# A decoder layer with 32 experts: the first 15 expert chunks are issued from GpSimd's queue, and the other chunk buffers are taken in another order

## The chip, the core and the metric

The kernel runs on one core of a Trainium2 chip. The metric is the time of one execution on the device, in microseconds (us). The median of three runs of the kernel before is 767.46 us (767.24 to 767.67). Engines are named as in the profile: PE is TensorE, PEld its weight loads, DVE is VectorE, ACT is ScalarE, POOL is GpSimd, SP is SyncE. A "q" behind a name (SPq) is the engine's instruction queue, from which DMAs are issued among other things.

## The reference, cut to what matters

One decoder layer on 512 tokens of width 1024. Three token mixers (attention over the 128 best keys that an indexer picks, a causal convolution, attention over 256 memory tokens) are projected, gated, added and multiplied by `w_o`. Behind them stands a mixture of 32 experts, of which each token takes two:

```
g_sel = argmax(h @ w_rg + b_rg)                    # one of 4 groups
top_v, top_i = top_k(e_in, 2)                      # 2 of its 8 experts
for n in range(N_EXPERTS):
    a, b = split(h @ w_up[n], 2)                   # w_up[n]: 1024 x 512
    out = out + combine[:, n] * ((silu(a) * b) @ w_down[n])   # w_down[n]: 256 x 1024
```

The weights of the experts are 32 x 6 chunks of 128 x 1024 numbers in float32, 512 KB each, some 100 MB in all. Every one of them is read once.

## The kernel before

**Stages.** `build` writes the program for all engines in source order; a scheduler then sets the order in each engine's queue by its own estimate of when an instruction can go, and puts in the waits. Each queue is worked off strictly in its order. The stages that matter here, with the time at which they run: attention A (`a_s1`, `a_s2`, lines 670 to 726) up to 414; its projection (`proj_units`, L441 to L449) up to 437; the output projection `w_o` (lines 841 to 857) up to 493; the router and the lists of tokens (lines 885 to 983) up to 512; and the experts (lines 1229 to 1252) to the end.

**Weights of the mixers** are loaded by `raw_w` (L132) on SP's queue into 3 buffers `w`; `split_w` cuts each into a high part `wh` (ACT, L127) and a low part `wl` (DVE, L128), with 3 buffers each. A load has to wait until the split of the chunk three before it has read its buffer.

**Expert chunks.** `seq` (L759) lists all 192 chunks in the order in which PE uses them: for each of 16 pairs of experts, three times two up chunks, the four down chunks of the pair before, and the last two up chunks. `slots` is a ring of 42 buffers of 512 KB, made from `RINGS` (L84): 6 of `w3`, 9 of `w1`, 4 of `ot`, 4 of `mg`, 3 of `w`, 3 of `wh`, 3 of `wl`, 2 of `xc`, 3 of `hw`, 2 of `hx`, 1 of `wg`, 2 of `s5`. Chunk n goes to slot n mod 42. These are no extra memory: each lies where earlier stages kept something, and its DMA waits until the last reader of that is done. `w3` (pool `rp`) lies over the queries, keys and values of attention A; `w1` (pool `ea`) over that stage's gates, scores and scratch; `ot` over the inputs of the projections; `mg` over the merged branches; `w`, `wh` and `wl` are the buffers of the mixers' weights; `xc` holds x for the residual; `hw` and `hx` the inputs of `w_o`; `wg` the router's scratch; `s5` what is written out per column of `w_o`.

**Who issues what.** `fetch` (L772) issues chunks, all from SP (L779): 23 at L805, ahead of the loop over `w_o`; 11 at L866, behind it; the rest of the first 42 at L1225, with `behind=first`, which makes the two `s5` chunks wait for the list of tokens (L777, a copy on POOL). From chunk 42 on, a chunk is issued when `expert_raw` asks for it, and waits until PE has used up the chunk 42 before it.

**POOL** does little: it raises to the power -0.5 (L146, L887), clears `zz` (L808; the matmul of L809 reads it) and two tiles for gathered tokens (L995), gathers each pair's tokens from `h2d` (L999), adds the results into the output (L1156) and loads one pair of chunks anew (L1197).

**Between `w_o` and the experts** PE runs `busy_pe(24)` (L983, matmuls of L863) ahead of the transposes of the first gathered tokens (L1137) and of the first up matmul (L1165).

Of the kernel before, what the change touches and what calls it, by code (L numbers as in the profile page):

```python
# [67 lines left out]
for _name, _w in (("g_mix", KD), ("g_mem", KD), ("b_gate", 24), ("conv_b", 4), ("ln_g", 4), ("ln_b", 4),  # L68
# [11 lines left out]
RING = 3  # L80
RING_A = 9
RING_B = 6
SPLIT = 3
RINGS = (("w3", RING_B), ("w1", RING_A), ("ot", 4), ("mg", 4), ("w", RING), ("wh", SPLIT), ("wl", SPLIT), ("xc", 2),  # L84
         ("hw", 3), ("hx", 2), ("wg", 1), ("s5", 2))
CONV_LOW = 1500
TOPK_LOW = 900

# [1 line left out]
def build(nc, tc, I, O, dbg=None):  # L90
    V, A, G, T, SY = nc.vector, nc.scalar, nc.gpsimd, nc.tensor, nc.sync
    es = ExitStack()
    with es:
# [36 lines left out]
        def raw_w(*key):  # L130
            w = wpool.tile([P, 1024], F32, name="w", tag="w")
            SY.dma_start(w, I["wp"][W_KEYS.index(key)])  # L132
            return w

        def split_w(w, n=1024):
            wh = spool.tile([P, 1024], F32R, name="wh", tag="wh")
            wl = spool.tile([P, 1024], F32R, name="wl", tag="wl")
            split_into(wh[:, :n], wl[:, :n], w[:, :n])
            return wh, wl
# [113 lines left out]
        for k in range(KD):  # L253
# [14 lines left out]
            wh, wl = split_w(kv_raw[k] if k < RING else raw_w("kv", k))  # L268
# [477 lines left out]
        def expert_at(e):  # L746
            return nc.values_load(ordi[0:1, e:e + 1], engines=(mybir.EngineType.SP,), min_val=0, max_val=NE - 1,
                                  skip_runtime_bounds_check_because="an index of 32 values")

        def chunk(e, c):  # L750

            if e in EARLY:
                return I["we"][e, c]
            if e not in at_pos:
                at_pos[e] = expert_at(e)
            return I["we"][bass.ds(at_pos[e], 1), c].rearrange("o p n -> (o p) n")
# [8 lines left out]
            if j is not None and j != NW:  # L765
                seq += [(e, 3) for e in pair(j)]
        pools = dict(ot=hp, hw=hp, hx=hp, w3=rp, xc=rp, w1=ea, w=wpool, wh=spool, wl=spool, s5=ea, wg=ea, mg=mpool)
        slots = [tag for tag, n in RINGS for _ in range(n)]
        bufs = {tag: slots.count(tag) for tag in slots}
        fetched, used = [], [0]  # L770

        def fetch(count, behind=None):  # L772
            for n in range(len(fetched), min(len(fetched) + count, len(seq))):
                tag = slots[n % len(slots)]
                w = pools[tag].tile([P, 1024], F32, name="we", tag=tag, bufs=bufs[tag])
                if behind is not None and tag == "s5":
                    G.tensor_copy(w[:, 0:1], behind[:, 0:1])  # L777
                e, c = seq[n]
                SY.dma_start(w, chunk(e, c))  # L779
                fetched.append(w)  # L780

        def expert_raw(e, c):
            n = used[0]
            assert seq[n] == (e, c)
            used[0] += 1
            if len(fetched) <= n:
                fetch(n + 1 - len(fetched))
            w, fetched[n] = fetched[n], None
            return w

        def eat(tag, name, bufs=1, dt=F32):
            return ea.tile([P, 1024], dt, name=name, tag=tag, bufs=bufs)
# [10 lines left out]
        out_v = O["out"][0:S, :].rearrange("(t p) d -> p t d", p=P)  # L803
        h2d_v = h2d.rearrange("(t p) d -> p t d", p=P)
        fetch(RING_B + RING_A + 4 + 4)  # L805
        lg = sct("lg")
        zz = eat("s4a", "zz")
        G.memset(zz[:, 0:148], 0.0)  # L808
        T.matmul(lg[:, 0:148], zz[:, 0:P], zz[:, 0:148], start=True, stop=False)  # L809
        lists = pvt("lists")  # L810

# [29 lines left out]
        for c in range(KD):  # L841
            ps = mmt("wo")
            wh, wl = split_w(wo_raw[c])
# [20 lines left out]

        busy_pe(5, xs[:, 512:1024])
        fetch(RING + 2 * SPLIT + 2)  # L866


# [4 lines left out]
        def r3(name, *dims, at=None, dt=F32):  # L873
            n = int(np.prod(dims))
            if at is None:
                at = taken[0]
                taken[0] += n
            assert at + n <= 1024
            t_ = scr[:, at:at + n]
            if dt is not F32:  # L880
                t_ = t_.bitcast(dt)
            ax = " ".join(f"a{i}" for i in range(len(dims)))
            return t_, t_.rearrange(f"p ({ax}) -> p {ax}", **{f"a{i}": d_ for i, d_ in enumerate(dims)})
# [4 lines left out]
        _, L = r3("lgs", NT, 36)  # L888
# [6 lines left out]
        _, pr = r3("pr", NT, NG)  # L895
# [13 lines left out]
        _, oh = r3("oh", NT, 2, NE)  # L909
# [15 lines left out]
        _, rk = r3("rk", NT, 2, NE)  # L925
# [476 lines left out]
```

## Time and profile before

| | us |
|---|---|
| median of 3 runs | 767.46 |
| the profiled execution | 766.1 |
| its span, from the first to the last instruction | 764.2 |
| PE busy | 717.2 (94%) |
| DVE busy | 477.5 (62%) |
| ACT busy | 266.3 (35%) |
| POOL busy | 90.8 (12%) |
| bytes by SP's DMA queue (q1) | 147.74 MB |
| bytes by POOL's DMA queue (q0) | 8.46 MB |

Busy time of PE is an upper bound of its work, since the ends of matmuls are modelled and a matmul that overlaps the next counts in full. The DMA share is the mean busy share of 16 DMA engines; it can come out a little above 1. All times within the span count from its start.

### The profile page before, as it was taken

How to read it: one execution, taken by the hardware profiler on the slowest of the kernel's cores; microseconds unless marked ns; L12 is line 12 of the kernel's file. 1: busy time of each engine (PE TensorE's matmuls, PEld its weight loads, DVE VectorE, ACT ScalarE, POOL GpSimd, SP SyncE). 2: the span in 40 equal slices, each digit the busy share in tenths (PEclk: the TensorE clock that was granted, in tenths of full speed). 3: DMA queues.
4: the chain of work that ended last, by engine and by line, in shares of the span. 5: the costliest groups of instructions: out<-in, count | busy, mean ns of one | idle time of the engine just before them, and what ended most of it. 6: DMA issues, size and time to landing. Idle time of an engine off the chain costs nothing. (4 is left out here: it accounts for less than half of the span.)

```text
span 764.2 us, 10080 instructions
## 1 busy us (share of the span) xinstructions
PE 717.2 (94%) x3468; PEld 477.9 (63%) x3468; DVE 477.5 (62%) x1085; ACT 266.3 (35%) x503; POOL 90.8 (12%) x82
## 2 busy tenths in 40 slices
PE   6999999999999999999998999989999998889882
PEld 5778888887878778888776888834333333233220
DVE  5879989999999999999986844272112112111100
ACT  6722254455633376237775422101111111000100
POOL 1110010011000050000000000021226322100010
PEclk9999999999999999999999999999999999999997
DMA  9632221213222222321214799999999999999982
GB/s 357 232 121 82 88 79 55 82 58 111 83 83 83 83 84 72 98 80 55 84 55 150 273 378 340 329 315 377 400 378 359 354 370 387 361 381 395 391 324 49
DMA packets 56684, 161.13 MB, mean 211 GB/s; under 512 B 9508, under 2 KB 17956, under 8 KB 56624
## 3 DMA queue, kind: packets, MB, share of 16 engines
q1 hardware_dynamic: 42320, 147.74, 52.2%
q0 software_dynamic: 6624, 8.46, 4.8%
q10 hardware_dynamic: 7680, 4.20, 1.9%
q8 instruction: 29, 0.48, 0.2%
q14 instruction: 31, 0.25, 0.1%
HBM read 162.93 MB, written 13.11 MB: 230 GB/s over the span
## 5 line engine op out<-in xcount | busy, mean ns | idle before, releaser
L1165 PE MATMUL up<-we,xt 128*64 128x512 f32 x544 | 140.8, 599 | 5.4 <-DMA we<-in_we 5.4
L127 ACT CAST wh<-w 128x1024 fp32r<-128x1024 f32 (+2 forms) x75 | 78.3, 1046 | 80.4 <-PE proj L314 22.2
L128 DVE TENSOR_TENSOR wl<-w,wh 128x1024 fp32r<-128x1024 f32 (+2 forms) x75 | 90.9, 1213 | 13.0 <-ACT wh L127 11.2
L1165 PEld LDWEIGHTS up<-we,xt 128*64 128x64 f32 x544 | 39.1, 136 | 77.5 <-issue 59.1
L328 DVE SCALAR_TENSOR_TENSOR y<-u,conv_wh,y 128x512 f32<-128x512 f32 x120 | 84.2, 745 | 0.3
L1155 DVE COPY y<-dn 128x512 f32<-128x512 f32 x17 | 11.8, 692 | 108.9 <-PE dn L1179 108.9
L1179 PE MATMUL dn<-we,acth 128*64 128x512 f32 x272 | 73.5, 596 | 0.6 <-issue 0.6
L314 PE MATMUL gate<-h,wh 128*128 128x512 f32 x240 | 67.9, 397 | 0.0
L1154 ACT COPY y<-dn 128x512 f32<-128x512 f32 x17 | 10.0, 586 | 123.7 <-PE dn L1179 72.7
L1179 PEld LDWEIGHTS dn<-we,acth 128*64 128x64 f32 x272 | 24.0, 137 | 44.9 <-issue 36.3
L314 PEld LDWEIGHTS gate<-h,wh 128*128 128x128 f32 x240 | 44.4, 188 | 9.5
L1156 POOL DMA_INDIRECT out<-y,midx x16 | 25.4, 1585 | 147.5 <-DVE y L1155 106.5
L314 PE MATMUL gate<-h,wl 128*128 128x512 f32 x120 | 34.7, 399 | 0.0
L314 PE MATMUL mm<-h,wh 128*128 128x512 f32 x120 | 32.7, 397 | 0.0
L422 ACT ACTIVATE gt<-gate,bgate 128x512 f32<-128x512 f32 x24 | 16.5, 686 | 39.8 <-PE gate L314 39.5
L1138 ACT COPY xt<-xtr 128x512 f32<-128x512 f32 x18 | 10.4, 585 | 56.4 <-PE xtr L1137 52.4
L1173 DVE COPY acth<-atr 128x256 f32<-128x256 f32 x17 | 7.2, 425 | 36.0 <-PE atr L1171 28.4
L1148 DVE SCALAR_TENSOR_TENSOR acts<-up,mwt,acts 128x256 f32<-128x256 f32 x16 | 7.7, 484 | 32.3 <-ACT acts L1147 29.6
L604 DVE MAX8 v<-score 128x8 f32<-128x256 f32 (+2 forms) x48 | 26.6, 557 | 0.8
L605 DVE MATCH_REPLACE8 score<-v,score 128x256 f32<-128x256 f32 (+2 forms) x48 | 26.0, 542 | 0.0
L314 PEld LDWEIGHTS gate<-h,wl 128*128 128x128 f32 x120 | 22.4, 188 | 5.4 <-issue 0.5
L314 PEld LDWEIGHTS mm<-h,wh 128*128 128x128 f32 x120 | 22.4, 188 | 5.1
(400 smaller groups left out, 1442.0 us busy)
## 6 DMA issues: line engine op xcount, KB each, us to landing
we<-in_we SPq DMA_DIRECT2D x192, 512.0 KB
w<-in_wp SPq DMA_DIRECT2D x75, 512.0 KB
x<-in_x SPq DMA_DIRECT2D x4, 512.0 KB
xr<-in_xt SPq DMA_DIRECT2D x4, 512.0 KB
out<-x1t ACTq DMA_DIRECT2D x8, 256.0 KB
h2d<-x1t ACTq DMA_DIRECT2D x6, 256.0 KB
m<-in_memt SPq DMA_DIRECT2D x2, 512.0 KB
m<-in_mem SPq DMA_DIRECT2D x2, 512.0 KB
```

The lines of the kernel that those rows point to most:

```text
L127: A.copy(wh, w)
L128: V.tensor_sub(wl, w, wh.bitcast(F32))
L314: T.matmul(ps, a[:, k * P:(k + 1) * P], b[k], start=(a is wh and b is rh and k == 0), stop=(b is rl and k == n - 1))
L328: V.scalar_tensor_tensor(Y[c], U[c][:, j:j + S], w, Y[c], op0=ALU.mult, op1=ALU.add)
L422: A.activation(t, ps, AF.Tanh, scale=0.5, bias=bgate[:, b * 8 + c:b * 8 + c + 1])
L604: V.max(v8, sel[t])
L605: V.match_replace(sel[t], v8, sel[t], GONE)
L1138: (A.copy if i or j == 0 else V.tensor_copy)(xt[i], ps.bitcast(F32))
L1155: V.tensor_copy(y[:, 512:1024], yp[1])
L1156: G.indirect_dma_start(out=O["out"], out_offset=bass.IndirectOffsetOnAxis(ap=ix[:, col:col + 1], axis=0), in_=y, in_offset=None, bounds_ch ...
L1165: T.matmul(ps[h * CAP:(h + 1) * CAP], xt[k // 4][:, o + h * CAP:o + (h + 1) * CAP], ws[h][:, i * 512:(i + 1) * 512], start=(k == 0), stop= ...
L1179: T.matmul(yp[n][h * CAP:(h + 1) * CAP], at[:, f * P + h * CAP:f * P + (h + 1) * CAP], ws[h][:, n * 512:(n + 1) * 512], start=(f == 0), st ...
```

## The change

Three edits. The ring is written out as a list: its first 26 places are as before, and the 16 others are put in the order `wh, wl, xc, wh, wl, wh, wl, hw, hw, hw, hx, hx, xc, wg, s5, s5` in place of three `wh`, three `wl`, two `xc`, three `hw`, two `hx`, `wg`, two `s5`. The first 15 chunks (those in `w3` and `w1`) are issued by GpSimd and all others by SP as before. And `zz` is cleared by VectorE, no longer by GpSimd.

```
-RINGS = (("w3", RING_B), ("w1", RING_A), ("ot", 4), ("mg", 4), ("w", RING), ("wh", SPLIT), ("wl", SPLIT), ("xc", 2),
-         ("hw", 3), ("hx", 2), ("wg", 1), ("s5", 2))
+SLOTS = (["w3"] * RING_B + ["w1"] * RING_A + ["ot"] * 4 + ["mg"] * 4 + ["w"] * RING + ["wh", "wl", "xc", "wh", "wl"]
+         + ["wh", "wl"] + ["hw"] * 3 + ["hx"] * 2 + ["xc", "wg", "s5", "s5"])
...
-        slots = [tag for tag, n in RINGS for _ in range(n)]
+        slots = SLOTS
...
-                SY.dma_start(w, chunk(e, c))
+                (G if n < RING_B + RING_A else SY).dma_start(w, chunk(e, c))
...
-        G.memset(zz[:, 0:148], 0.0)
+        V.memset(zz[:, 0:148], 0.0)
```

## Rows read from the trace of the kernel before

**Rows 1.** Stages: start:end, length, busy time of engines, PEclk, DMA share, GB/s.
```profile
362.00:414.30 52.30, 51.67 (x252) 40.15 (x251) 46.71 (x132) 38.74 (x82) 0.00 (x0) 1.00 0.20 65
414.30:437.00 22.70, 20.44 (x88) 16.20 (x87) 16.94 (x26) 8.23 (x12) 1.12 (x2) 1.00 0.81 300
437.00:493.20 56.20, 56.20 (x293) 46.99 (x291) 23.97 (x34) 15.25 (x22) 0.95 (x1) 1.00 0.98 348
493.20:512.20 19.00, 15.65 (x102) 8.56 (x101) 15.17 (x89) 2.26 (x6) 3.67 (x6) 0.91 0.95 330
...
522.00:686.00 164.00, 157.43 (x792) 58.71 (x790) 29.81 (x60) 20.13 (x37) 44.55 (x37) 1.00 1.01 376
686.00:743.00 57.00, 49.51 (x176) 15.91 (x172) 6.04 (x11) 4.72 (x9) 4.68 (x3) 1.00 1.00 382
```

**Rows 2.** Chain that ended last: start us, us, what; five DMA pieces in a row.
```profile
686.78 10.12 DMA we<-in_we
...
730.51 12.47 DMA we<-in_we
```

**Rows 3.** DMA issues from 413 to 512, by line.
```profile
we<-in_we SPq DMA_DIRECT2D x42, 512.0 KB
```

**Rows 4.** SP's queue around the first use: start us, us, merged instructions.
```profile
503.17 6.11 SPq L779 DMA_DIRECT2D we<-in_we  x3
...
514.18 2.07 SPq L779 DMA_DIRECT2D we<-in_we  x3
```

**Rows 5.** What SP waited for from 509.5 to 522.5: total, times, longest.
```profile
SPq L779 <- PE up L1165: 7.7, 3, 4.9
```

**Rows 6.** PE from 503 to 516 in order of time.
```profile
504.33 6.92 PE L863 MATMUL junk<-soh 128*128 128x512 f16 x24
510.90 0.98 PE L1137 MATMUL xtr<-identr,xg 128*128 128x128 f32 x8
...
512.22 3.65 PE L1165 MATMUL up<-we,xt 128*64 128x512 f32 x16
```

**Rows 7.** PE at the end of attention A; the bracket is its wait and what ended it.
```profile
417.19 0.73 PE L314 MATMUL proj<-oah,wh 128*128 128x512 f32 x2 [2.26 <-ACT oah L715]
```

**Rows 8.** SP's queue from 400 to 470, parts of it.
```profile
414.31 1.98 SPq L779 DMA_DIRECT2D we<-in_we  x4
424.50 0.33 SPq L132 DMA_DIRECT2D w<-in_wp  x1
...
453.71 6.49 SPq L779 DMA_DIRECT2D we<-in_we  x6
```

**Rows 9.** Last readers of old tiles, one line each: count, ns min/median/max, first to last start.
```profile
L707 PE MATMUL pva<-pal,vs x20: 391/407/503, 346.4 to 414.4; 128*128 128x512 f32 x20
...
L449 DVE TENSOR_TENSOR mg<-mg,gt x16: 673/682/693, 319.0 to 439.7; 128x512 f32<-128x512 f32 x16
```

**Rows 10.** POOL from 250 to 520 in order of time, parts of it.
```profile
275.96 5.29 POOL L146 TENSOR_TENSOR rsa<-rsa,nhalf 128x8 f32<-128x8 f32 x1 [2.56 <-DVE rsa L145]
289.61 1.01 POOL L146 TENSOR_TENSOR rc<-rc,nhalf 128x4 f32<-128x4 f32 x1 [8.36 <-DVE rc L145]
429.30 0.22 POOL L808 MEMSET zz<- 128x148 f32 x1 [138.69 <-DVE mg L449]
...
490.72 0.95 POOL L995 MEMSET xg<- 128x1024 f32 x1 [60.30 <-PE tr L816]
...
505.68 1.24 POOL L999 DMA_INDIRECT xg<-h2d,fidx  x1 [7.85 <-DVE other L1018]
```

**Rows 11.** Chunk DMAs by what issues them, over the whole span: ns min/median/max.
```profile
L779 SPq DMA_DIRECT2D we<-in_we x192: 237/333/954, 414.3 to 738.0; - x192
...
L1197 POOL DMA_INDIRECT we<-in_we,xrow x12: 989/993/1043, 571.4 to 593.1; - x12
```

**Rows 12.** DVE's scaling of attention weights, by form.
```profile
L690 DVE TENSOR_SCALAR pa<-pa,la x32: 271/380/491, 339.7 to 407.0; 128x128 f32<-128x128 f32 x8, 128x256 f32<-128x256 f32 x8, 128x384 f32<-128x384 f32 x8, 128x512 f32<-128x512 f32 x8
```

**Rows 13.** DVE's split of a weight at the end of attention A, in order of time.
```profile
411.70 1.23 DVE L128 TENSOR_TENSOR wl<-w,wh 128x1024 fp32r<-128x1024 f32 x1
```

## What was predicted

> **What bounds the kernel now.** I read the stages first, then the chain that ended last, then the DMA issues ahead of the first expert matmul, then SP's and PE's queues around that moment.
>
> The stages show two regimes [rows 1]. Up to 493 PE sets the pace: 51.67 of 52.30 us busy from 362 to 414.3, and 56.20 of 56.20 from 437 to 493.2. From 522 on the DMA engines do: share 1.01 and 1.00, while PE has gaps (157.43 of 164, 49.51 of 57). The chain ends in five DMAs of chunks one behind the other, the first 10.12 us, the last 12.47 us from 730.51 [rows 2]. So the end is the start of the saturated stream plus what is left to load at that moment. A reader may stop here and conclude that DMAs have to start earlier, since the DMA engines stand at a share of 0.20 from 362 to 414.3 and 0.81 up to 437. The next rows say why that is not enough.
>
> The ring has 42 places. From 413 to 512 SP issues exactly 42 chunks [rows 3]; the last three of them go from 503.17 to 509.28, and the next chunk goes at 514.18 [rows 4]. In that stretch SP waits for PE's up matmuls, 7.7 us in three waits, the longest 4.9 us [rows 5]: every place is taken, and a place comes free only when PE has used a chunk. PE's first up matmul starts at 512.22 [rows 6]. So the stream that bounds the end begins at PE's start on the experts, with the same 42 chunks done and the same 150 to come, however early the first ones were fetched.
>
> What sets 512.22? From 414.3 to 437 PE is idle for 2.26 us, and all of that is one wait for attention A's last result on ACT; from there to 493 it has no gap [rows 1, 7]. Then follow the router's chain on DVE and 24 matmuls that fill time, 504.33 for 6.92 us, back to back with the transposes at 510.90 [rows 6]. The first gather, issued at 505.68 [rows 10], is in by then, as PE shows no wait for it. No expert chunk stands in that chain.
>
> **The change part by part.** The sum is made against the profiled execution: span 764.2 us, 766.1 us with what lies around it. That is 1.36 us under the median of the runs, so a difference found here is added to 767.46.
>
> *SP loses 15 chunks.* They stand in SP's queue between weight loads, for example four at 414.31, then a load of `w` at 424.50 [rows 8]. The last of the ring's first 15 are among the six issued from 453.71 on, so they are out by 460.2 at the latest. SP saves 15 x 0.33 us (0.24 to 0.95 us each [rows 11]) = 5.0 us of issuing, and the loads of `w` behind them lose a neighbour. It gives PE nothing, as PE waits for no load between 417.19 and 493.2 [rows 1]. Value 0.
>
> *POOL gains 15 DMAs.* No row shows POOL issuing a plain copy. Nearest are its indirect loads of the same 512 KB, 0.99 us each; the lower bound is SP's 0.24 us, the upper bound 5.29 us, which a POOL instruction of 1.01 us took at 275.96 beside a busy DVE [rows 10, 11]. I take 0.99: 14.9 us in all. The places come free at different times: the values of attention A have their last reader at 414.4 + 0.5, two gates at 439.7 + 0.68 [rows 9]. If POOL takes the chunks in the order of the ring, the last eight or so wait behind the gates until 440.4 and then go one behind the other: 440.4 + 8 x 0.99 = 448.3, at the upper bound 482.7. Queued behind them on POOL: the clearing of one gather tile (its first reader is the gather at 505.68 or the next), that of the other, now at 490.72, and the router's power behind it [rows 10]. Before the change POOL stood idle for 138.69 us up to 429.30 and 60.30 us up to 490.72, so all of it is covered, even at the upper bound. Landing at 482.7 plus the 12.47 us that a DMA took in the queue's depth [rows 2] is 495, still 17 us ahead of PE's first use. Value 0, bounds 0 and 0 for this path; what POOL's work may cost DVE is a rival below.
>
> *The 16 other places in another order.* Chunk n still waits for chunk n - 42, and the last places (`wg`, `s5`) still come free when the router and the lists are done. In the order of SP's queue the scheduler had already interleaved them by readiness. At best chunks 26 to 38 land a few us sooner and the DMA engines then stand idle just ahead of 512, where they now show a share of 0.95. Value 0.
>
> *`zz` on DVE.* POOL took 0.22 us [rows 10]; DVE has 5.76 us idle between 414.3 and 437 and 32 us behind that [rows 1]. Value 0, and up to 0.2 us if it falls into the chain.
>
> Sum: 0, with 0.2 us of room. 767.46 rounds to 767.4.
>
> **The rivals.**
>
> *A, faster: the idle DMA time is won back.* This holds if the stream were bound by DMA from its first chunk. Idle between 414.3 and 512.2 [rows 1]: 0.19 x 22.7 + 0.02 x 56.2 + 0.05 x 19 = 6.4 us, so 761.0; if chunks also fill the time ahead of 414, at most 15 x 0.524 MB / 376 GB/s = 20.9 us, 746.5. Against it stand the 42 chunks and SP's wait for PE [rows 3 to 5]. It decides only where places are still empty at 512. Chance 0.07.
>
> *B, faster: PE reaches the experts sooner.* Either the 2.26 us wait [rows 7] shrinks because the new order of instructions is kinder, or the first gather, with fewer chunks in its way, lands sooner and was the limit after all. The second is worth at most 510.90 - 506.92 (end of its issue) = 4.0 us. For it: a start on the experts that moves moves the end by the same amount. Against: PE shows no wait for the gather. Priced at half, 2 us: 765.5. Chance 0.12.
>
> *C, slower: POOL's issuing holds up DVE in attention A.* By the layout four places of the ring are free before attention A ends, and POOL would work for up to 4 x 1.24 us = 5.0 us beside DVE, which is busy 46.71 of 52.30 us there [rows 1]. If DVE stands still as long, the wait at 414.4 grows and everything behind it moves: up to 772.5. It decides if a DVE instruction that has the form with the higher rate (L690, 512 columns in 0.49 us, where L449 takes 0.68 us [rows 9, 12]) falls on a POOL instruction. Against: beside the POOL instruction of 5.29 us it was POOL that waited. Chance 0.09.
>
> The Trainium skill, "SBUF — State Buffer", section "SBUF: two separate sides", speaks against the change: it says that GpSimd writes the descriptors of its DMAs through a port pair that DVE's faster modes lock, that whoever comes first keeps it for a whole instruction while the other fully blocks, and that a plain load does better on SP's queue. By that rule the loads come late (which the 17 us above cover) or DVE does (C). The trace shows the first kind of wait, 5.29 us [rows 10]; no row shows the second.
>
> *D, slower: the scheduler's order shifts.* A split on DVE of 1.23 us already lies in the last steps of attention A [rows 13]; one or two more there cost 1.2 to 2.5 us: 768.7 to 769.9. Chance 0.04.
>
> *E: the change does not do what it says.* POOL holds seven or eight chunks behind the two gates, and the loads come hardly earlier than from SP. By the argument above that costs nothing either; it lies within the forecast.
>
> **How the numbers follow.** Under 0.2% (1.5 us) is about what a measurement of this kernel cannot tell from no change. The forecast, E included, has 0.68, with a range of its own from 766.5 to 768.6 for the 0.2 us above and small shifts of order. Faster by over 0.2%: A and B, 0.07 + 0.12 = 0.19. Slower: C and D, 0.09 + 0.04 = 0.13. The range reaches over B's price and D's: 765.2 to 770.0. Outside are A and the larger part of C, some 0.14.
>
> **What would show it.** Right: 15 DMAs on POOL at L779 ahead of 460, and 27 on SP's queue between 413 and 512; the first up matmul at 512 within 0.5 us; SP's wait for PE's up matmuls behind chunk 41 as long or longer; a higher DMA share up to 437 and a lower one from 493 to 512; shares of 1.0 again from 522. Wrong: a first up matmul that moved, with PE's wait at 417 or a wait for the gather having changed (B, C, D); or an up matmul at the same 512 and an earlier end (A), which would mean that the ring was not what held the stream back.

## The result and the profile after

The changed kernel takes 776.06 us (median of 4 runs, 773.40 to 776.88), where the kernel before took 767.57 beside it (4 runs): a ratio of 1.0097, with a 95% interval from 1.0075 to 1.0118. By the medians it is slower by 8.5 us (the ratio stands for 7.4 us, 5.8 to 9.1), and the time lies 6 us above the range of the prediction. One execution of a3 (3960 us) and one of b1 (1428 us) below, far outside all others, are left out of their ratios. The profiled execution is the one of 776.88 us, with a span of 775.1.

The same stages as in [rows 1], with the same columns, after the change:

```profile
362.00:414.30 52.30, 52.13 (x258) 41.00 (x256) 46.84 (x139) 39.78 (x83) 2.45 (x4) 1.00 0.31 111
414.30:437.00 22.70, 19.98 (x80) 15.36 (x79) 15.26 (x23) 8.05 (x13) 1.59 (x3) 0.92 0.59 211
437.00:493.20 56.20, 52.96 (x255) 43.99 (x254) 24.84 (x34) 14.73 (x21) 5.21 (x9) 0.94 0.84 301
...
522.00:686.00 164.00, 158.55 (x848) 60.26 (x844) 30.86 (x64) 22.20 (x40) 45.30 (x39) 0.99 1.00 372
686.00:743.00 57.00, 49.81 (x184) 16.09 (x182) 7.09 (x13) 5.08 (x10) 5.86 (x4) 1.00 1.02 386
```

The third line holds the loss. Before, PE had no gap from 437 to 493.2 and a granted clock of 1.00; now it works 52.96 of 56.20 us and the clock is 0.94. The expert stream from 522 on is saturated as before (1.00 and 1.02). So the stage that the prediction called covered is the one that lost time, and the stage that sets the end only starts later: the first up matmul, at 512.22 in [rows 6], now starts at 522.25.

```profile
522.25 3.65 PE L1165 MATMUL up<-we,xt 128*64 128x512 f32 x16
```

What stood around PE's gap, from the order of work of all engines (start us, us, engine, line, what; the bracket is the idle time ahead of it and what ended it):

```profile
472.67 0.59 ACT L821 COPY x1t<-tr 128x512 f32<-128x512 f32 x1 [6.25 <-DMA h2d<-x1t]
...
473.29 0.69 DVE L823 TENSOR_TENSOR x1t<-tr,gB 128x512 f32<-128x512 f32 x1 [6.15 <-ACT x1t L821]
473.90 0.68 DVE L849 TENSOR_TENSOR x1c<-wo,xr 128x512 f32<-128x512 f32 x1
...
474.63 0.64 PE L834 MATMUL lg<-gwr,x1c 128*128 128x36 f32 x2 [3.24 <-DVE x1c L849]
```

Read it from the bottom. PE waits 3.24 us for `x1c`, which DVE adds at L849. DVE is not late with that addition: it stands in DVE's queue behind the other half of `x1t` (L823), which stands behind ACT's half (L821), and ACT waited 6.25 us for a transfer. `x1t` has two buffers (`s5`), each of which is written out by two DMAs of ACT's queue, to `out` and to `h2d`, and can be written again only when both have left. So a write to memory for which nobody asks before the experts has become a wait of PE, by way of a buffer and of two in-order queues. Around the end of PE's gap the clock falls to half, for 6.8 us:

```profile
473.90:480.70 6.80, 6.07 (x21) 5.30 (x22) 3.19 (x5) 2.12 (x3) 0.00 (x0) 0.50 0.88 276
```

Why the transfer was late, from POOL's and SP's queues and the table of DMA issues (last column: median us from issue to landing):

```profile
417.37 1.59 POOL L779 DMA_DIRECT2D we<-in_we  x3 [7.66 <-PE pva L707]
444.31 4.24 POOL L779 DMA_DIRECT2D we<-in_we  x8 [25.35 <-DVE mg L449]
...
440.72 1.28 SPq L779 DMA_DIRECT2D we<-in_we  x3
445.60 1.53 SPq L779 DMA_DIRECT2D we<-in_we  x2
```

```profile
we<-in_we POOLq DMA_DIRECT2D x8, 512.0 KB, 15.8
we<-in_we SPq DMA_DIRECT2D x6, 512.0 KB, 9.6
...
out<-x1t ACTq DMA_DIRECT2D x1, 256.0 KB, 14.5
h2d<-x1t ACTq DMA_DIRECT2D x1, 256.0 KB, 18.6
```

POOL's eight chunks, held behind the last gate, leave in 4.24 us, while SP, rid of them, reaches its next places earlier and issues six chunks and two loads of `w` from 440 to 452. By the prediction's reading of [rows 8] SP was still issuing chunks of the first 15 at 453.71. The first writes of `x1t`, issued at 453.17 and 454.01, land 14.5 and 18.6 us later; 454.01 + 18.6 = 472.6 is where ACT goes on. With SP issuing all chunks (run a1 below, writes issued at 451.77 and 452.61) the same two took 5.2 and 5.1 us:

```profile
out<-x1t ACTq DMA_DIRECT2D x1, 256.0 KB, 5.2
h2d<-x1t ACTq DMA_DIRECT2D x1, 256.0 KB, 5.1
```

How the DMA engines divided their time from 456 to 468, by queue (packets, MB, share of 16 engines), first after, then before:

```profile
q0 software_dynamic: 689, 2.49, 51.1%
q1 hardware_dynamic: 701, 2.09, 43.2%
q10 hardware_dynamic: 651, 0.33, 9.0%
```

```profile
q1 hardware_dynamic: 1002, 3.59, 75.3%
q10 hardware_dynamic: 1751, 0.87, 24.5%
```

The queue that appears with POOL's chunks is q0; q10 carries ACT's writes (0.33 MB / 651 = 0.5 KB in a packet), q1 SP's loads. With three queues full, each moves nearly the same number of packets: 689, 701, 651. For ACT, with packets a seventh as long (q0's are 2.49 MB / 689 = 3.6 KB), that is 0.33 MB in 12 us, where it moved 0.87 MB with SP alone beside it. The counts before are not equal (1002 and 1751): from 464 to 468 ACT's queue moved 1386 packets and SP's 173, as SP had issued nothing since 460.2. So that window doesn't test an equal share.

Smaller pieces stand elsewhere. From 19.9 to 26.7 the clock is at half, and attention A's last matmul starts at 416.56 where it started at 414.44: 2.1 us later, and the fall lies long before POOL's first chunk at 364.9. From 419.2 to 422.7 the clock is at half once more, which the trace of before doesn't have. And behind the last write of the output the program ends later: POOL's last drain is longer (the third figure is the longest in ns).

```profile
L1398 POOLq DRAIN  x3: 50/103/5050, 769.2 to 774.8; - x3
```

### The profile page after: what moved, and what is told of

The parts are those of the page before. It is cut to its first block, busy times and chain, and to the rows that moved or that the text cites. A ratio compares the mean times of both kernels' runs of the same rounds, so it can differ in the third digit from the quotient of the medians.

```text
span 775.1 us, 10076 instructions
## 1 busy us (share of the span) xinstructions
PE 722.1 (93%) x3468; PEld 481.9 (62%) x3468; DVE 477.6 (62%) x1086; ACT 266.4 (34%) x503; POOL 101.4 (13%) x96
## 5 line engine op out<-in xcount | busy, mean ns | idle before, releaser
L127 ACT CAST wh<-w 128x1024 fp32r<-128x1024 f32 (+2 forms) x75 | 78.3, 1046 | 79.6 <-PE proj L314 22.5
L128 DVE TENSOR_TENSOR wl<-w,wh 128x1024 fp32r<-128x1024 f32 (+2 forms) x75 | 90.9, 1213 | 13.4 <-ACT wh L127 12.4
L779 POOL DMA_DIRECT2D we<-in_we x15 | 8.3, 558 | 147.5 <-ACT oah L715 72.1
```

Source lines behind the costliest of these rows:

```text
L127: A.copy(wh, w)
L128: V.tensor_sub(wl, w, wh.bitcast(F32))
```

## Experiments

**Theories.** T1: POOL's burst on top of SP's chunks delays ACT's writes of `x1t`; ACT, DVE and PE wait in turn, and the clock falls behind PE's gap. T2: POOL's issuing holds up DVE in attention A (rival C of the prediction). T3: the other order of places does it. T4: the clock falls by chance. The later theories T5 to T8 are named in the expectations where they are put to the test. Each ratio below is against the kernel before, run beside it.

**The change in parts.** Edits to the changed kernel:

```
a1_order   SY.dma_start(w, chunk(e, c)), and zz again on G
a2_queue   slots = [tag for tag, n in RINGS for _ in range(n)]   # old order of places
a3_pool6   (G if n < RING_B else SY).dma_start(...)              # the six w3 chunks
a4_pool9   (G if RING_B <= n < RING_B + RING_A else SY).dma_start(...)   # the nine w1 chunks
```

> The new order of the ring alone: SP issues all chunks again and GpSimd clears zz as before. Theory T1 (the eight chunks that GpSimd lets go together at 444 to 448, on top of eight of SP, fill the DMA engines, so that the writes of x1t land late, ACT waits 6.2 us for one of their buffers, PE waits 3.2 us, and TensorE's clock falls behind it): as the kernel before, 767.5 within 1 us, and ACT's wait for x1t's buffers at 0. Rival T2 (GpSimd's issuing holds up DVE in attention A): also 767.5. Rival T3 (the order of the places makes chunks or writes late): 774 to 777. Rival T4 (the lower clock is chance of the runs): anything from 767 to 777.

Measured: 768.47 us, ratio 1.0009 (0.9997 to 1.0021). PE has no gap from 437 to 493.2, and ACT waits for no write at L821. A wait of 3.8 us at L127, behind a late issue of a write of `x1t`, is in the kernel before too (3.9 us).

> The 15 chunks on GpSimd and zz on VectorE, with the old order of the ring. T1 and T2: 773 to 777 as the changed kernel; T1 with ACT waiting about 6 us for a write of x1t and PE 3 us for x1c. T3: 767.5 within 1 us.

Measured: 776.69 us, ratio 1.0121 (1.0092 to 1.0150). ACT waits 5.8 us for `h2d<-x1t`, PE 2.8 us for `x1c`.

> The changed kernel with 6 of the 15 chunks (the places w3) on GpSimd, and the 9 of w1 on SP. No chunk on GpSimd waits for the gates then, so nothing is let go together at 444. T1: 767 to 769, ACT's wait for the writes under 1 us. T2: as slow as the changed kernel, 773 to 777, since these six are the ones that GpSimd issues beside attention A. T4: anything.

Measured: 768.57 us, ratio 1.0008 (0.9989 to 1.0028). No wait of ACT for a write of `x1t`, PE 56.20 of 56.20.

> The complement: the 9 chunks of w1 on GpSimd, the 6 of w3 on SP. The eight that wait for the gates go together as in the changed kernel. T1: 773 to 777, ACT's wait about 6 us, PE's 3 us. T2: 767 to 769, since GpSimd issues at most one chunk beside attention A.

Measured: 776.50 us, ratio 1.0103 (1.0083 to 1.0123). ACT waits 6.7 us, PE 3.7 us:

```profile
444.03 4.29 POOL L779 DMA_DIRECT2D we<-in_we  x8 [32.51 <-DVE mg L449]
...
ACT x1t L821 <- DMA h2d<-x1t: 6.7, 1, 6.7
PE lg L834 <- DVE x1c L849: 3.7, 1, 3.7
```

The order of places is worth nothing (T3 falls). The six chunks that POOL issues beside attention A cost nothing either (T2 falls); the nine, eight of which go in one burst at 444, cost as much as all 15. In a1 and a3 the clock also fell to half behind the wait at 417, and they are not slower, so that fall is not the loss. No run lets eight chunks go in one burst from SP's queue, so how much of the lateness is the burst and how much the third queue stays open.

**Take away the wait, double the dose, spread the burst, look again.** Edits to the changed kernel:

```
b1_third   RING_A = 8; one more "s5" in SLOTS; ys = eat("s5", "x1t", 3)
b2_pool23  (G if n < RING_B + RING_A + 8 else SY).dma_start(...)
b3_spaced  if 8 <= n < RING_B + RING_A:
               for _ in range(3): G.memset(w, 0.0)     # ahead of the DMA
b4_after   the changed kernel as it is
```

> The changed kernel, but one of the nine w1 places of the ring becomes a third x1t buffer (tag s5), so POOL issues 14 chunks, seven of them at once behind the gates, and ACT may write x1t three times before it needs the first transfer to have landed. T1 (the burst makes the x1t writes land 14 to 18 us late, ACT waits 6 us for one of them, PE waits 3 us, and TensorE's clock halves for 6.8 us behind PE's gap): the writes still land late, but ACT's wait for h2d<-x1t at L821 falls from 6.2 to under 1.5 us, PE's wait for x1c at L849 from 3.2 to about 0.8, no half clock near 474, first up matmul near 514.5; 768 to 770 us. Rival T5 (what is late is the loads of w or xr behind the burst, or POOL's queue itself takes something from PE): the x1t wait goes but another takes its place, 774 to 777.

Measured: 769.15 us, ratio 1.0034 (1.0022 to 1.0046). The writes are as late as ever, 14.5 and 17.4 us, and seven chunks still go in one burst; but ACT waits for none of them, and PE and clock are whole from 437 to 493.2. The first up matmul starts at 516.47, not 514.5: this trace has a half clock from 20.4 to 27.3, and attention A's last matmul starts at 417.07.

```profile
out<-x1t ACTq DMA_DIRECT2D x1, 256.0 KB, 14.5
h2d<-x1t ACTq DMA_DIRECT2D x1, 256.0 KB, 17.4
...
437.00:493.20 56.20, 56.20 (x287) 46.88 (x286) 27.54 (x39) 16.35 (x23) 4.68 (x8) 1.00 0.91 318
```

So the late write costs nothing where its buffer isn't wanted back. That the loads behind the burst are what hurts (T5) falls with it.

> The changed kernel with POOL issuing the first 23 chunks rather than 15, so that 16 stand in one burst behind the gates. T1: the x1t writes land later still (18 us or more after their issue), ACT waits 6 to 10 us, PE 3 to 7 us, half clock behind it; 776 to 781 us. T5b (the wait depends only on POOL's burst of eight, not on the number of chunks in flight): as the changed kernel, 775 to 777.

Measured: 775.48 us, ratio 1.0121 (1.0102 to 1.0140), under T1's lower end of 776. ACT waits 7.4 us and PE 4.4 us, a little over the changed kernel's 6.2 and 3.2: T1's direction, but the time can't tell the two doses apart and lies where T5b had it. Nor were the 16 one burst. Behind the last gate POOL issued five chunks from 441.70, then six singly up to 456.27, nearly each of these behind the landing of an earlier chunk:

```profile
447.93 0.54 POOL L779 DMA_DIRECT2D we<-in_we  x1 [2.04 <-DMA we<-in_we]
450.79 0.54 POOL L779 DMA_DIRECT2D we<-in_we  x1 [2.33 <-DMA we<-in_we]
```

The bytes of chunks and loads in this stretch hardly grew either: from 437 to 475 the queues of POOL and SP together moved 11.1 MB here and 11.0 MB in the changed kernel. So the dose was not doubled, and T5b is not refuted.

> The changed kernel, still 15 chunks from POOL, but ahead of each of the last seven POOL clears its place three times (about 3 x 0.95 us), so that the burst becomes one chunk each 3.4 us or so, from 444 to 468. T1: x1t writes land within 5 to 9 us, no wait of ACT over 1.5 us that PE feels, no gap of PE over 1.5 us from 437 to 493, no half clock near 474; 767 to 770 us, though 15 chunks still come from POOL and land later than in the changed kernel. Rival T5 (POOL as issuer is at fault, by its port or by the queues that its transfers take): 774 to 777 as the changed kernel, or more by the clearing.

Measured: 770.16 us, ratio 1.0037 (1.0012 to 1.0062), 0.2 us over T1's upper end. All 15 chunks still come from POOL; the last seven didn't go one by one, but mostly in pairs some 6.4 us apart, the last at 470.77. ACT's wait has shrunk to a rest, and PE feels nothing:

```profile
ACT x1t L824 <- DMA h2d<-x1t: 1.0, 1, 1.0
...
437.00:493.20 56.20, 56.20 (x282) 46.72 (x281) 28.87 (x42) 17.09 (x24) 24.07 (x30) 1.00 0.92 325
```

The first writes of `x1t` still take 12.3 and 13.4 us here, not the 5 to 9 expected. That gives the limit. In the changed kernel ACT writes `x1t` at 452.56 and 459.44, every 6.9 us, so it wants the first buffer back at 466.3; its last write was issued at 454.01. A landing within 12.3 us is free; 18.6 us costs ACT 6.3, and 13.4 us costs it about one.

> The changed kernel again, for a second trace. T1: the same wait of ACT for h2d<-x1t (5.5 to 7 us), PE's wait for x1c of 3 to 4.5 us and the half clock behind it come again, 774 to 777; the half clock at 19.9 and at 419 us, which I hold for chance, may be absent, and then the first up matmul starts near 519 to 520 rather than 522.25. T4 (the clock falls by chance and makes most of the difference): no wait of PE, or the half clock at another place; 768 to 777 by how often it falls.

Measured: 776.15 us, ratio 1.0123 (1.0104 to 1.0143). ACT waits 6.0 us, PE 3.0 us, the clock is at half from 472.8 to 479.7; there is no half clock near 20, and the first up matmul starts at 519.80. What recurs is the wait and the fall with it; the early fall was chance, as the same kernel has it in one trace and not in the other.

**What the clock takes, and whether the end follows PE.** The same edit in the changed kernel (c1) and in the kernel before (c2), in the loop over c, ahead of L834:

```
                if c == 4 and k == 4:
                    junk = mmt("junk")
                    for _ in range(12):
                        T.matmul(junk, wh[:, 0:P], mgh[0], start=True, stop=True)
```

> The changed kernel with 12 matmuls that nothing needs, of 0.23 us each (2.8 us), right ahead of the logits for which PE waits 3 to 4.5 us for x1c at L849. They fill PE's gap and leave ACT's wait for h2d<-x1t (near 6 us) as it is. T1 (the half clock for 6.8 us near 474 follows from PE's gap): gap under 1.5 us, granted clock 1.00 from 437 to 493, and since half speed for 6.8 us costs 3.4 us, 771.5 to 773.5 us. T4 (the clock falls for another reason, such as the DMA load or chance): it falls near 474 all the same, 775 to 777. T6 (the clock is all of it and the wait itself costs nothing): 768 to 770.

Measured: 772.13 us, ratio 1.0072 (1.0046 to 1.0098). ACT waits 6.0 us as ever, PE 0.2 us, and the clock stays at 1.00:

```profile
468.70 2.96 PE L848 MATMUL junk<-mh,wh 128*128 128x512 f32 x12
471.87 1.08 PE L834 MATMUL lg<-gwr,x1c 128*128 128x36 f32 x8 [0.20 <-DVE x1c L853]
...
437.00:493.20 56.20, 55.99 (x283) 46.38 (x283) 24.56 (x36) 14.77 (x21) 5.21 (x9) 1.00 0.92 320
```

Work that nobody needs, put where PE would wait, makes the changed kernel some 3.9 us faster (ratios of 1.0072 and 1.0123 from two sets of runs, so good to about 2.5 us). The fall of the clock follows from PE's gap, then: the filler takes the place of the gap, and what is won is the clock. That fits the 3.4 us which half speed for 6.8 us costs by reckoning, about as much as the gap itself. T4 falls for this stretch, and T6 with it, since the time stays over 770.

> The kernel before with the same 12 matmuls at the same place, where PE has no gap: PE's work grows by 12 x 0.23 = 2.8 us between attention A and the experts, and nothing else changes. T1 and the prediction's own model (the end follows PE's start on the experts one for one): first up matmul and end 2.8 us later, 770 to 771 us. T7 (the experts' stream makes up for a later start, since more chunks are there by then): 767 to 769.

Measured: 770.31 us, ratio 1.0052 (1.0033 to 1.0070), that is 4.0 us (2.5 to 5.4). In the traces the first up matmul and the span are at 516.19 and 768.2 us, against 513.26 and 765.6 in d1 below: 2.9 and 2.6 later for 2.8 us of work. The end follows PE's start on the experts about one for one, as the prediction's model had it, and T7 falls.

> The kernel before once more, for a second trace of it, to see what the half-speed stretches near 20 and near 417 us are, which most traces of the other kernels show and the first trace of this one doesn't. If they are chance (T1): a time of 766 to 769, a ratio of 1.00, and at least one of the two stretches here too, with no wait of PE from 437 to 493. If POOL's issuing brings them: neither of them here, as in the first trace.

Measured: 767.91 us, ratio 0.9999 (0.9987 to 1.0011). The half clock near 417 is here too (418.6 to 422.1), the one near 20 isn't. Of the 14 traces 12 show the fall behind the 2.3 us wait at 417, in kernels that lose time and in those that don't. The prediction's trace of before is one of the two without it.

**The end of the program.** b1 and b3 have no gap and no fall from 437 to 493.2 and are still 2.6 and 2.8 us slower than before. The longest drain of POOL at the end grows with the DMAs that POOL has issued: 3817 ns with 46 (before), 4315 with 52 (a3), 4560 with 55 (a4), 5050 with 61 (after). To measure that by itself, in the kernel before:

```
        spare = eat("s4b", "spare", 2)
        for i in range(30):
            G.dma_start(spare[:, i * 8:i * 8 + 8],
                        I["gf"][:, i * 8:i * 8 + 8].to_broadcast([P, 8]))
```

> The kernel before (all chunks from SP) with 30 more plain DMAs from POOL, each of 4 KB (128 rows of 32 bytes), ahead of the clearing of the gather tiles, in POOL's idle time near 430 to 490. They move next to no data. In the traces so far POOL's last drain takes 3817 ns with 46 POOL DMAs, 4315 with 52, 4560 with 55, 5050 with 61, 5703 with 69, and the semaphore instruction ahead of it 1108 to 1580 ns: about 82 and 20 ns more for each DMA. T8 (the end of the program costs 0.10 us for each DMA that POOL has issued, whatever it moved): the drain takes 6.27 us, the semaphore instruction 1.7 us, first up matmul at 512 to 514 as before, time +3.1 us: 770 to 771.5. Rival (it goes with the bytes or with the load at the end of the stream): drain near 3.8 us, time 767 to 768.5.

Measured: 787.85 us, ratio 1.0265 (1.0241 to 1.0289). On the end of the program T8 was right to the row:

```profile
L1401 POOLq DRAIN  x3: 50/103/6275, 780.4 to 787.2; - x3
...
L1299 POOLq INC_SWDGE_SEM  x1: 1720/1720/1720, 778.6 to 778.6; - x1
```

From 3817 to 6275 and from 1108 to 1720 ns for 30 DMAs is 0.10 us each, with next to no bytes. The time lies 16 us above T8's range and further above the rival's, and the first up matmul starts at 532.89, not at 512 to 514. Late writes of `x1t` are in this again, larger. The table from 445 to 475, and the waits from 437 to 493.2:

```profile
q0 software_dynamic: 767, 0.10, 49.4%
q1 hardware_dynamic: 1374, 4.73, 42.2%
q10 hardware_dynamic: 1070, 0.99, 9.5%
...
out<-x1t ACTq DMA_DIRECT2D x2, 256.0 KB, 21.1
...
h2d<-x1t ACTq DMA_DIRECT2D x1, 256.0 KB, 26.1
```

```profile
PE lg L837 <- DVE x1c L852: 15.3, 2, 13.4
...
ACT x1t L824 <- DMA h2d<-x1t: 5.6, 2, 4.6
```

POOL's queue moved 0.10 MB and took half of the DMA engines' time. The first `h2d<-x1t`, issued at 457.47, landed after 26.1 us, at 483.6, which ended ACT's wait of 4.6 us to write `x1t` again; PE stood still for 13.4 us, and its clock was at half for 13.6 us, from within the gap (477.4 to 491.0). Ahead of that ACT had stood for 16.7 us at issuing the writes of the second buffer, the last of them at 476.99, when the first `out<-x1t` (451.81 + 25.1) had landed. Other transfers were as late, a load of `w` 24.9 us, so this run doesn't show how much of the 13.4 us the writes alone make.

## Why the prediction was wrong

**What held.** The bound was read rightly: 27 of the 42 places were issued by SP and 15 by POOL, the stream from 522 is saturated, and a later start of PE moves the end by as much (c2). POOL held eight chunks behind the gates, as said. The order of places and `zz` on DVE were worth nothing (a1; a3 has `zz` on DVE).

**Small slips in the working** change none of this. The sums 767.46, 761.06 and 746.56 are cut to 767.4, 761.0 and 746.5, not rounded. The 5.29 us of POOL at 275.96 is set against 1.01 us of an instruction half its size [rows 10]; the same form took 1.64 us at 264.30. That the difference is a lock held by DVE is argued, not shown.

**The step that failed** is *POOL gains 15 DMAs*, with its "Value 0, bounds 0 and 0 for this path", and with it *SP loses 15 chunks*. POOL's issuing was even cheaper than the 0.99 us each that it took (8.3 us for the 15, the eight done by 448.5 where it had 448.3). It asked when POOL would have issued, which of POOL's own later work stood behind that, and when the chunks would land, and found all of it covered. It counted the chunks' landing only against the chunks' first use. The prediction did not ask which other transfers share the DMA engines from 444 to 470, and what comes free when those land. A row was at hand: the stage from 437 to 493 had a DMA share of 0.98 [rows 1], so what is issued sooner there can push something else back. ACT's writes in the same stretch had two buffers and, by the working under b3, 12.3 us of room; the first `h2d<-x1t` took 18.6. The term that the prediction put at 0 came to some 8 us: about 3 of PE's wait, 3.4 of the clock, 1.5 at the end of the program. The argument "PE waits for no load" was true of loads; the transfer that came late is a store.

**The cost, term by term.** b4 against d1, two traces with the same falls of the clock up to 437: the span grows by 9.1 us (774.7 to 765.6).

- PE's wait: 3.0 us.
- The clock behind it at half for 6.8 us: 3.4 us. From attention A's last matmul to the last of the logits' matmuls takes 89.7 us in place of 83.3, which is these two.
- The end of the program: (5050 - 3817) + (1420 - 1108) ns = 1.5 us for 15 DMAs.
- A rest of 1.2 us, most of it between the first up matmul and the last write of the output, 241.4 us against 240.1. That stretch takes 239.0 to 240.1 us in the 13 other traces, whatever the kernel, so I put no cause to it.

In the trace of the first measurement the early fall of the clock adds 2.1 us, the one behind the wait at 417 some 1.2 (the rest of 89.6 us against 81.7 from attention A's last matmul to the last logits), and the stretch of the experts gives 0.7 back. b1 and b3, without the first two terms, have 1.4 and 1.5 of their 2.6 and 2.8 us in the third; what remains, about 1 us, is within their intervals but for b1, and stays open.

**The rivals.** A fell: the DMA share from 414 to 437 went down, from 0.81 to 0.59, not up, since four chunks that SP issued there [rows 8] had left POOL by 409.2. B fell: PE's wait for attention A's last result stayed at 2.26 us, and PE shows no wait for the gather. C, the rival on the right side, fell by its mechanism: with POOL issuing two chunks at 364.9 and more at 395.7 and 409.2, DVE's scaling (L690) took 271/380/487 ns (least, median, most), as in [rows 12] but for 4 ns, and DVE's busy time to 414.3 is 46.84 us for 46.71. The rule of the Trainium skill, "SBUF — State Buffer", section "SBUF: two separate sides", that was weighed there is borne out by no run: issuing a chunk took POOL 537 to 767 ns in the changed kernel and at most 770 in any, beside a busy DVE too. D fell: PE, DVE and ACT keep their order but for `zz`. E came nearest to what happened, and was priced at nothing: eight chunks did stay behind the gates, but there they went in one burst of 4.24 us, where on SP's queue loads of `w` stand between the chunks [rows 8].

A rule that bears on this stands in the Trainium skill, "DMA: Bandwidth & Descriptors", section "Queues, rings and completion order": each DMA engine goes round the queues that have work, a packet of each in turn. The packets counted above for three full queues, 689, 701 and 651, agree, as far as the profile's packets (0.5 KB for ACT, one row of the write) are those that the page means. Had I weighed it, the sentence to draw would have been that a third full queue leaves ACT's writes a third of the packets and, at 0.5 KB against nearly 4, far less than a third of the bytes.

## What to carry to other kernels

Before a transfer is moved to another queue or sooner, list what else is in flight where it will now land, stores included, and for each the buffer that it gives back and who waits for that buffer: the room is (buffers x period) less the time to issue, here 12.3 us. A burst can be spread, or the one buffer that runs short given a third copy, and then lateness costs nothing. A short gap of PE should be priced at its own length and half that of the fall of the clock that comes with it, here 3 and 3.4 us, and a DMA moved to POOL at 0.10 us at the end of the program, where nothing here covered it.

## What the hardware showed that was not expected

- From 456 to 468 the queues shared the DMA engines by packets, not by bytes: with three full, 0.33 MB went through ACT's queue in 12 us beside 2.49 and 2.09 MB. In d2 packets of some 0.13 KB (0.10 MB / 767) took 49.4% of the engines' time over 30 us, 0.31 us each (0.494 x 16 x 30 us / 767), while POOL's chunk packets took 0.14 us each (0.511 x 16 x 12 us / 689) for 3.6 KB.
- The drain of POOL at the end takes 82 ns, and the semaphore instruction ahead of it 20 ns, for each DMA that POOL issued in the program, whatever it moved: nearly the same step from 46 to 52, 55, 60, 61, 69 and 76 DMAs (82 to 83 ns; 20 to 22 ns).
- A gap of PE of 2.8 to 4.4 us near 470 came with half clock for 6.8 us, from within or right behind the gap, in each of the five traces that had one (after, a2, a4, b2, b4), and a gap of 13.4 us with half clock for 13.6. Where matmuls that nothing needs filled the gap the clock stayed at 1.00.
